# Short products of constants ahead of the small products of a chunked recurrence

## The chip, the core and the metric

The kernel runs on one core of one Trainium2 chip. The metric is the device time of one execution in microseconds. A core has a matrix engine (TensorE, PE in the profile, its weight loads PEld), three engines for elementwise work (VectorE: DVE, ScalarE: ACT, GpSimd: POOL) and a queue that issues the transfers (SyncE: SP). Each engine works through its own instructions in order and waits on semaphores for the others. PE writes only to PSUM, which is cut into banks of 512 float32 columns; before a bank is written again, what stands in it must have been read.

## What is computed

One step of a decoder layer for 576 tokens (64 of 8 short samples and 512 of a prompt): a norm, one wide projection, two kinds of token mixer side by side (a state-space mixer, and RWKV-7 with 16 heads of 64), an output projection, a gated feed-forward block, and an embedding per layer. The change touches the RWKV-7 part, whose recurrence is

```
def wkv_scan(r, decay, k, v, kk, a, s0):
    ...
    def step(s, inp):
        r_t, w_t, k_t, v_t, kk_t, a_t = inp
        s_kk = jnp.einsum('bhvk,bhk->bhv', s, kk_t)
        s = (s * w_t[:, :, None, :] - s_kk[..., None] * (kk_t * a_t)[:, :, None, :]
             + v_t[..., None] * k_t[:, :, None, :])
        return s, jnp.einsum('bhvk,bhk->bhv', s, r_t)

    s_fin, out = lax.scan(step, s0.astype(f32), seq)
```

All products are in float32 accuracy: a large one is split into a high and a low part of both operands and run as three products (L213 to L215).

## The kernel before

The 576 columns are cut into 9 chunks of 64 (chunk 0 holds the samples), and the 16 heads into four quarters of four heads: two pairs (`jj`) of two heads (`e`), the two heads of a pair in the upper and lower 64 partitions. For each quarter the kernel runs these steps.

- `prep` (L509): the decays, the normalised keys and the scaled operands `G` and `BK`. Its `by_channel` (L489) turns a factor per token into one per channel with PE transposes (L503, L506) into a bank `cb` (one buffer) or, in `head_norm`, `cx` (two buffers).
- `start_states` (L706): loads the samples' states and multiplies them with chunk 0's operands into `cb` (L714), 32 small products for each pair.
- `gram` (L581): the products of all operands within a chunk (L593), in five groups; a group fills a tile `lin` of two banks (two buffers), and DVE, ACT and POOL mask and copy it out (L603 to L618).
- `solve` (L632): inverts 72 triangular blocks with 60 dependent operations on DVE (L654, L656), between transfers through DRAM.
- `combine` (L661): puts the blocks' inverses together with 64 products of 32 x 32 (L678, L692) in two tiles `cx`.
- `chain` (L719): nine steps `core` (L769, L777, L782), `prompt_state` (L801) and `outp` (L792), each step needing the state of the one before it.
- `head_norm` (L866): centres the output (L879), sums its squares by token (L476) and scales it.

Beside this, `fill` takes projections off a list: each is 48 wide products of 288 columns (L213 to L215) into a `lin` tile. A projection is written where the quarter's steps call for it, but a scheduler orders all instructions of an engine by its own model of their times when the program is built; so wide products come to stand between the small ones of the chain. Tiles with one or two buffers decide when a product can start: the tile before it in the same buffer must have been read.

`gmask` is a constant of 128 x 128 ones and zeros in bfloat16 (L145), `blk` and `ident` are float32 constants.

Of the kernel before, what the change touches and what calls it, by code (L numbers as in the profile page):

```python
# [56 lines left out]
    return [8 + 2 * q, 9 + 2 * q, 2 * q, 2 * q + 1, 16 + 2 * q, 17 + 2 * q]  # L57


CONV_BC = [8, 9, 10, 11]  # L60
CONV_X = [0, 1, 2, 3, 4, 5, 6, 7]

# [12 lines left out]
def hybrid_step(ctx, tc, A):  # L75
# [168 lines left out]
    sst = se.tile([P, 26, 9], F32, tag="sst", name="sst")  # L244
    nc.sync.dma_start(sst[:], A["s_shift"])
    sho = se.tile([P, 26, 9], F32, tag="sho", name="sho")

    def cx_ps():
        return bank(sq_, "cx", 2)
# [239 lines left out]
    def by_channel(rn, jj, psum, tag):  # L489

        rnv = rn[:].rearrange("p (w h) -> p w h", w=5)[:, :, jj * 2:jj * 2 + 2].unsqueeze(3)
        if tag:
            rx = sp.tile([P, 5, 2, 64], F32, tag=tag, name=nm(tag), bufs=1)
            V.tensor_copy(rx[:], rnv.to_broadcast([P, 5, 2, 64]))
            rx4 = rx[:, 4]
        else:
            rx = slot("rx", [P, 4, 2, 64])
            V.tensor_copy(rx[:], rnv[:, 0:4].to_broadcast([P, 4, 2, 64]))
            rx4 = s2.tile([P, 2, 64], F32, tag="rx4", name=nm("rx4"))
            V.tensor_copy(rx4[:], rnv[:, 4].to_broadcast([P, 2, 64]))  # L500
        ps = psum()
        for w, a in enumerate(WIN[:4]):
            T.transpose(ps[:, a:a + P], rx[:, w].rearrange("p a b -> p (a b)"), ident[:])  # L503
        yield 0, 448, ps[:, 0:448]
        ps = psum()
        T.transpose(ps[:, 0:P], rx4.rearrange("p a b -> p (a b)"), ident[:])  # L506
        yield 448, NT, ps[:, 0:P]

# [72 lines left out]
    def gram(s):  # L581

        s.Lst = s2.tile([P, 9, 2, 64], F32, tag="Lst", name=nm("Lst"))
        for gs in ((0,), (1, 2), (3, 4), (5, 6), (7, 8)):
            n = len(gs)
            gl = slice(gs[0], gs[0] + n)
            mk = dgmask if gs[0] == 0 else gmask
            ps = lin.tile([P, 1024], F32, tag="lin", name=nm("lin"))
            for i, g in enumerate(gs):
                for jj in jj2:  # L590
                    for e in range(2):
                        c = e * 512 + (2 * i + jj) * 128
                        T.matmul(ps[:, c:c + 128].rearrange("p (a t) -> p a t", a=2),  # L593
                                 s.BK[jj][H[e], g].rearrange("p a t -> p (a t)"),
                                 s.G[H[e], g, jj, :, e], start=True, stop=True)
# [65 lines left out]
    def combine(s):  # L661
# [3 lines left out]
        for e in range(2):  # L665
            for z in range(2):
# [3 lines left out]
            nc.sync.dma_start(AA[e * 64:e * 64 + 32].rearrange("s g j t -> s (g j) t"),  # L670
                              s.Ad[e].rearrange("g s t -> s g t"))
        Wp = cx_ps()
        Wv = Wp[:].rearrange("p (g j t) -> p g j t", g=8, j=2)
        for g in range(1, 9):
            for jj in jj2:
# [4 lines left out]
        for e in range(2):  # L680
# [3 lines left out]
            else:  # L684
                V.tensor_scalar(AA[hi_:hi_ + 32, 1:9], Wv[hi_:hi_ + 32], -1.0, None, ALU.mult)
        Xp = cx_ps()
        Xv = Xp[:].rearrange("p (g j t) -> p g j t", g=8, j=2)
        for g in range(1, 9):
            for jj in jj2:
# [16 lines left out]
    def start_states(s):  # L706

        S0 = load_states(s)
        Zp = cb_ps()
        Zv = Zp[:, 0:256].rearrange("p (j a t) -> p j a t", j=2, a=2)  # L710
        for jj in jj2:
            for b in range(8):
                for e in range(2):
                    T.matmul(Zv[H[e], jj, :, b * 8:b * 8 + 8], S0[H[e], b, jj, :],  # L714
                             s.G[H[e], 0, jj, :, e, b * 8:b * 8 + 8], start=True, stop=True)
        s.Z = sp.tile([P, 2, 2, 64], F32, tag="Z", name=nm("Z"))
        act(s.Z[:], Zv)

    def chain(s):  # L719
# [45 lines left out]
        def core(g):  # L765
# [6 lines left out]
            V.tensor_copy(xs[H[1]], xw[H[1], :, 1])  # L772
            ups = cx_ps()
            uw = ups[:].rearrange("p (j v) -> p j v", j=8)
            for jj in jj2:
                for e in range(2):
                    T.matmul(uw[H[e], jj, :], TT[H[e], g, jj, :], xs[H[e], jj, :], start=True, stop=True)  # L777
# [747 lines left out]
```

## Time and profile before

| | us |
|---|---|
| timed runs, median of 3 | 1366.8 (1364.27 to 1370.2) |
| profiled execution, its own time | 1370.43 |
| span of its trace, first to last instruction | 1368.7 |
| mean granted clock of TensorE | 0.947 of full |
| first quarter's gram ends, combine begins | 138.7, 190.4 |
| first chain, first to last step begins | 198.9 to 305.5 |
| second chain | 349.8 to 450.8 |
| third chain | 486.1 to 563.6 |
| fourth chain | 595.8 to 671.2 |

The steps of the chains are found in the trace by L769, those of the gram by L593, those of the combine by L678 and L692, each four times over. Behind 671 us the state-space mixer and the output projection end, and from about 825 us on there are only wide products. A plain float32 product stands in the trace as two rows, one of the split kind as one. A row's duration holds the way through the array as well, so two rows in a row overlap; what a product costs in a stream is the distance of two starts. `PEclk` is the share of full speed that the clock of TensorE was granted.

### The profile page before, as it was taken

The page shows a single profiled execution, that of the slowest core. Times are in us where ns is not written, and L with a number is a line of the kernel's source. Part 1 is how long each engine was busy: PE and PEld are TensorE (multiplying, and loading weights), DVE is VectorE, ACT ScalarE, POOL GpSimd, SP SyncE. Part 2 cuts the span into 40 slices and gives each one's busy share as a digit, 9 for nine tenths or more (in the row PEclk, how much of TensorE's full clock was granted, in tenths as well). Part 3 has the DMA queues.
Part 4 walks back from the last instruction along what each step waited for, and adds up shares of the span by engine and source line. Part 5 has one row for each costly group of instructions (what it writes and reads, how often), then busy time and mean ns, then how long its engine had stood idle before and what let it go on. Part 6 is the DMA issues. An engine that isn't in the chain of part 4 may idle for free.

```text
span 1368.7 us, 26325 instructions
## 1 busy us (share of the span) xinstructions
PE 1259.1 (92%) x10565; PEld 1160.4 (85%) x10565; DVE 719.6 (53%) x1333; ACT 577.4 (42%) x1148; POOL 550.2 (40%) x543
## 2 busy tenths in 40 slices
PE   6897999999989979899989979999999999999986
PEld 5786897789868857777779769999999999999985
DVE  7648766787687785843367676522222221111255
ACT  6565345634653553344425364432332332222253
POOL 5326414632454153133456676432332332334332
PEclk9997899899979989989999989999999999999998
DMA  4322342234223312362644532233232222222432
GB/s 162 124 70 62 85 119 60 81 100 128 61 90 91 101 58 84 88 209 82 189 145 142 183 97 71 70 85 79 84 85 81 83 85 77 82 80 79 148 92 69
DMA packets 94458, 135.56 MB, mean 99 GB/s; under 512 B 34704, under 2 KB 39056, under 8 KB 94336
## 3 DMA queue, kind: packets, MB, share of 16 engines
q1 hardware_dynamic: 94336, 133.88, 32.8%
q8 instruction: 83, 1.36, 0.4%
q14 instruction: 39, 0.32, 0.1%
HBM read 106.10 MB, written 27.75 MB: 98 GB/s over the span
## 4 chain that ended last, share of the span: by engine, by line
PE 60%; DVE 15%; ACT 5%; DMA 5%; issue 4%; POOL 3%; DVEq 0%; SPq 0%; ACTq 0%; POOLq 0%
PE lin L215 16%; PE lin L213 16%; PE lin L214 16%; DVE h L375 2%; DVE Tt L656 1%; DVE tmp L654 1%; DMA raw<-wts 1%; POOL wlo L198 1%; DVE suv L809 1%; PE cx L777 1%; PE lin L593 1%; PE cx L769 1%; DVE wlo L198 1%; PE cx L792 1%; DVE pg L1373 1%
## 5 line engine op out<-in xcount | busy, mean ns | idle before, releaser
L213 PE MATMUL lin<-xhi,whi 128*128 128x288 f32 (+1 forms) x1488 | 450.8, 303 | 3.3 <-ACT whi L92 2.2
L215 PE MATMUL lin<-xhi,wlo 128*128 128x288 f32 (+1 forms) x1488 | 447.9, 301 | 3.2 <-POOL wlo L198 2.2
L214 PE MATMUL lin<-xlo,whi 128*128 128x288 f32 (+1 forms) x1488 | 447.7, 301 | 1.0 <-POOL xlo L186 1.0
L198 POOL TENSOR_TENSOR wlo<-raw,whi 128x512 fp32r<-128x512 f32 x136 | 182.8, 1344 | 501.9 <-ACT whi L92 462.1
L92 ACT ACTIVATE whi<-raw 128x512 fp32r<-128x512 f32 (+1 forms) x272 | 168.8, 621 | 397.7 <-PE lin L214 341.1
L213 PEld LDWEIGHTS lin<-xhi,whi 128*128 128x128 f32 (+1 forms) x1488 | 281.4, 189 | 10.5 <-ACT whi L92 2.6
L215 PEld LDWEIGHTS lin<-xhi,wlo 128*128 128x128 f32 (+1 forms) x1488 | 282.3, 190 | 7.0 <-POOL wlo L198 2.8
L214 PEld LDWEIGHTS lin<-xlo,whi 128*128 128x128 f32 (+1 forms) x1488 | 281.9, 189 | 6.1 <-POOL xlo L186 2.1
L198 DVE TENSOR_TENSOR wlo<-raw,whi 128x512 fp32r<-128x512 f32 (+1 forms) x136 | 98.4, 724 | 167.4 <-ACT whi L92 164.8
L215 PE MATMUL lin<-ah,wlo 128*128 128x288 f32 x352 | 105.0, 298 | 0.9
L213 PE MATMUL lin<-ah,whi 128*128 128x288 f32 x352 | 104.0, 296 | 0.0
L214 PE MATMUL lin<-al,whi 128*128 128x288 f32 x352 | 103.8, 295 | 0.0
L215 PEld LDWEIGHTS lin<-ah,wlo 128*128 128x128 f32 x352 | 66.2, 188 | 3.2 <-POOL wlo L198 2.6
L214 PEld LDWEIGHTS lin<-al,whi 128*128 128x128 f32 x352 | 66.1, 188 | 0.0
L213 PEld LDWEIGHTS lin<-ah,whi 128*128 128x128 f32 x352 | 66.0, 187 | 0.0
L1332 DVE TENSOR_TENSOR sg<-lin,sg 128x576 f32<-128x576 f32 x22 | 16.7, 758 | 82.9 <-PE lin L215 81.7
L1327 DVE TENSOR_TENSOR sg<-lin,rstd 128x576 f32<-128x576 f32 x22 | 16.7, 758 | 69.3 <-PE lin L215 69.0
L654 DVE TENSOR_TENSOR tmp<-L,Tt 72x30 f32<-72x30 f32 (+14 forms) x120 | 48.9, 407 | 3.2
L656 DVE TENSOR_TENSOR Tt<-Tt,tmp 72x30 f32<-72x30 f32 (+14 forms) x120 | 46.1, 384 | 3.4
L213 PE MATMUL lin<-xu,whi 128*128 128x288 f32 x128 | 39.9, 313 | 8.5 <-ACT xu L92 6.9
L215 PE MATMUL lin<-xu,wlo 128*128 128x288 f32 x128 | 40.0, 314 | 7.3 <-DVE wlo L198 5.5
L186 POOL TENSOR_TENSOR al<-sg,ah 128x576 fp32r<-128x576 f32 x22 | 31.5, 1433 | 32.1 <-ACT ah L92 32.1
(370 smaller groups left out, 2513.6 us busy)
## 6 DMA issues: line engine op xcount, KB each, us to landing
raw<-wts SPq DMA_DIRECT2D x271, 256.0 KB, 2.6
S<-s_wkv SPq DMA_DIRECT2D x8, 512.0 KB, 5.1
hd<-s_ssm SPq DMA_DIRECT2D x8, 512.0 KB, 4.0
o_ssm_s<-hd SPq DMA_DIRECT2D x8, 512.0 KB, 2.9
xbc_d<-E SPq DMA_DIRECT2D x12, 288.0 KB, 2.1
x<-xT SPq DMA_DIRECT2D x8, 288.0 KB
gate_d<-g SPq DMA_DIRECT2D x8, 288.0 KB, 2.6
bv_d<-rw SPq DMA_DIRECT2D x8, 288.0 KB
```

The lines of the kernel that those rows point to most:

```text
L92: S.activation(out, in_, func, bias=bias, scale=scale)
L186: eng.tensor_tensor(lo[:], src, hi[:].bitcast(F32), ALU.subtract)
L198: eng.tensor_tensor(lo[:, 0:n], raw[:, 0:n], hi[:, 0:n].bitcast(F32), ALU.subtract)
L213: T.matmul(ps[:, a:b], whi, xhi[:, a:b], start=first, stop=False)
L214: T.matmul(ps[:, a:b], whi, xlo[:, a:b], start=False, stop=False)
L215: T.matmul(ps[:, a:b], wlo, xhi[:, a:b], start=False, stop=last)
L375: V.scalar_tensor_tensor(h[:], E[:, i:i + 600], w(i), h[:], ALU.mult, ALU.add)
L593: T.matmul(ps[:, c:c + 128].rearrange("p (a t) -> p a t", a=2), s.BK[jj][H[e], g].rearrange("p a t -> p (a t)"), s.G[H[e], g, jj, :, e], s ...
L654: V.tensor_tensor(o, L[:, jx:jx + 1, jx + 1:32].to_broadcast([NB, jx, n]), Tt[:, 0:jx, jx:jx + 1].to_broadcast([NB, jx, n]), ALU.mult)
L656: V.tensor_tensor(Tt[:, 0:jx, jx + 1:32], Tt[:, 0:jx, jx + 1:32], o, ALU.subtract)
L1327: V.tensor_tensor(s_[:], ps, rs[:], ALU.mult)
L1332: V.tensor_tensor(s_[:], up, s_[:], ALU.mult)
```

## The change

A helper `beat` multiplies `gmask` with a column of itself, spread over 512 columns, and writes the result into a tile that is about to be written by the step's own products; these begin with `start=True` and overwrite it. It has no operand that anything computes late, so it waits only for the tile's bank. The helper is called ahead of both sets of transposes in `by_channel` (one beat each), of each gram group (ten ahead of the first quarter's first group, two ahead of its others, three and one in the other quarters), of both products of `combine` (two each), of the states' products (two, and two of 256 columns between the pairs), and of the second product of the third quarter's last two chain steps (two each). That makes 107 products.

```
+BEATS = [(10, 2), (3, 1), (3, 1), (3, 1)]
...
+    def beat(ps, n=1, w=512):
+
+        for _ in range(n):
+            T.matmul(ps[:, 0:w], gmask[:].rearrange("p a b -> p (a b)"), gmask[:, 0, 0:1].to_broadcast([P, w]),
+                     start=True, stop=True)
...
         ps = psum()
+        beat(ps, 1)
         for w, a in enumerate(WIN[:4]):
             T.transpose(ps[:, a:a + P], rx[:, w].rearrange("p a b -> p (a b)"), ident[:])
         yield 0, 448, ps[:, 0:448]
         ps = psum()
+        beat(ps, 1)
         T.transpose(ps[:, 0:P], rx4.rearrange("p a b -> p (a b)"), ident[:])
...
             ps = lin.tile([P, 1024], F32, tag="lin", name=nm("lin"))
+            beat(ps, BEATS[s.q][bool(gs[0])])
             for i, g in enumerate(gs):
...
         Wp = cx_ps()
+        beat(Wp, 2)
...
         Xp = cx_ps()
+        beat(Xp, 2)
...
+        beat(Zp, 2)
         for jj in jj2:
+            if jj:
+                beat(Zp[:, 256:512], 2, 256)
             for b in range(8):
...
             ups = cx_ps()
             uw = ups[:].rearrange("p (j v) -> p j v", j=8)
+            if q == 2 and g > 6:
+                beat(ups, 2)
             for jj in jj2:
```

The scheduler decides where a beat stands, and it moves other products too. Three places on PE follow; in the changed kernel the beat is L252, and the other line numbers are 7 to 18 higher (L593 is L603, L714 is L729, L678 is L689, L503 is L511, L213 to L215 are L214 to L216).

First, PE in the second quarter, where the states' products into `cb` meet the first gram products into `lin`, before:

```order
L714 MATMUL cb_3081<-G_2686,S_456_3079 64x2x8 x17
L792 MATMUL cx_1824<-G_982,suv_1768 64x64
L714 MATMUL cb_3081<-G_2686,S_456_3079 64x2x8 x15
L593 MATMUL lin_3117<-G_2686,bk_2849 128x128
L801 MATMUL cx_1840<-suv_1768,bkt_1811 64x64 x4
L792 MATMUL cx_1824<-G_982,suv_1768 64x64 x3
L593 MATMUL lin_3132<-G_2686,bk_2849 128x128 x2
```

and the same place on PE after the change:

```order
L252 LDWEIGHTS gmask
L252 MATMUL cb_3119<-gmask 128x256
L729 MATMUL cb_3119<-G_2720,S_456_3117 64x2x8
L809 MATMUL cx_1854<-G_982,suv_1798 64x64
L729 MATMUL cb_3119<-G_2720,S_456_3117 64x2x8 x5
L818 MATMUL cx_1870<-suv_1798,bkt_1841 64x64 x4
L809 MATMUL cx_1854<-G_982,suv_1798 64x64 x3
L729 MATMUL cb_3119<-G_2720,S_456_3117 64x2x8 x10
L603 MATMUL lin_3159<-G_2720,bk_2885 128x128
L252 LDWEIGHTS gmask
L252 MATMUL lin_3177<-gmask 128x512
L603 MATMUL lin_3177<-G_2720,bk_2885 128x128 x2
```

The beats stand between the two pairs' products and ahead of the group's first product; a weight load of `gmask` stands as a row of its own.

Second, PE in the head norm of the second quarter, where the second pair's factors are transposed into `cx` (`rxg` is the factor per token; `ulh` and `ull` belong to the small projections of the fourth quarter's preparation), before:

```order
L213 MATMUL lin_6071<-ulh_345,whi_5973 128x288
L503 MATMUL cx_3824<-ident,rxg_3822 128x128 x4
L506 MATMUL cx_3830<-ident,rxg_3822 128x128
L214 MATMUL lin_6071<-ull_346,whi_5973 128x288
L215 MATMUL lin_6071<-ulh_345,wlo_5974 128x288
```

and after the change:

```order
L252 LDWEIGHTS gmask
L252 MATMUL cx_3879<-gmask 128x512
L214 MATMUL lin_5984<-xhi_456,whi_6017 128x288
L252 LDWEIGHTS gmask
L252 MATMUL cx_3886<-gmask 128x512
L215 MATMUL lin_5984<-xlo_457,whi_6017 128x288
L216 MATMUL lin_5984<-xhi_456,wlo_6018 128x288
L214 MATMUL lin_5984<-xhi_461,whi_6017 128x288
L215 MATMUL lin_5984<-xlo_462,whi_6017 128x288
L216 MATMUL lin_5984<-xhi_461,wlo_6018 128x288
L511 MATMUL cx_3879<-ident,rxg_3877 128x128 x4
L515 MATMUL cx_3886<-ident,rxg_3877 128x128
```

Before, the projections from the layer's input (`xhi`, `xlo`) were through by then and only the small ones (`ulh`, `ull`) were left; now the former stand there. Counted over the whole of PE's order, 128 products of 288 columns (L213 to L215) stand between the last step of the second chain and the first of the third before, and 194 after; behind the first step of the third chain there are 12 more (of the small projections); between the last step of the first chain and the last step of the second there are 78 fewer.

Third, PE at the combine of the fourth quarter (`AA` and `Lst` are its operands), before:

```order
L503 MATMUL cx_5547<-ident,rxg_5545 128x128 x4
L506 MATMUL cx_5553<-ident,rxg_5545 128x128
L740 MATMUL tr_6735<-ident,rw_5893 128x128
L740 MATMUL tr_6735<-ident,rw_5961 128x128
L678 MATMUL cx_6545<-AA_6538,Lst_6153 32x32 x32
```

and after:

```order
L511 MATMUL cx_5629<-ident,rxg_5627 128x128 x4
L515 MATMUL cx_5636<-ident,rxg_5627 128x128
L764 MATMUL tr_6791<-ident,bk_6136 128x128
L764 MATMUL tr_6791<-ident,bk_6193 128x128
L755 MATMUL tr_6838<-ident,rw_5977 128x128
L755 MATMUL tr_6838<-ident,rw_6045 128x128
L252 LDWEIGHTS gmask
L252 MATMUL cx_6644<-gmask 128x512
L252 LDWEIGHTS gmask
L252 MATMUL cx_6644<-gmask 128x512
L689 MATMUL cx_6644<-AA_6637,Lst_6245 32x32 x32
```

Two beats stand between the last transposes and the combine's first product, and two of the transposes (L764) have moved behind the head norm's.

More of the change, by code (lines that the diff above doesn't have):

```diff
@@ L246, in hybrid_step, with beat @@
     sho = se.tile([P, 26, 9], F32, tag="sho", name="sho")
+    def beat(ps, n=1, w=512):
+        for _ in range(n):
+            T.matmul(ps[:, 0:w], gmask[:].rearrange("p a b -> p (a b)"), gmask[:, 0, 0:1].to_broadcast([P, w]),
+                     start=True, stop=True)
     def cx_ps():
@@ L501, in by_channel @@
         ps = psum()
+        beat(ps, 1)
         for w, a in enumerate(WIN[:4]):
@@ L672, in combine @@
         Wp = cx_ps()
+        beat(Wp, 2)
         Wv = Wp[:].rearrange("p (g j t) -> p g j t", g=8, j=2)
@@ L686, in combine @@
         Xp = cx_ps()
+        beat(Xp, 2)
         Xv = Xp[:].rearrange("p (g j t) -> p g j t", g=8, j=2)
@@ L774, in core @@
             uw = ups[:].rearrange("p (j v) -> p j v", j=8)
+            if q == 2 and g > 6:
+                beat(ups, 2)
             for jj in jj2:
```

6 lines of the change are left out of this document (added).

## The prediction

> **What bounds the kernel now.** I read four views in this order: the page, the busy time by stretch, the chain of waits, and the order of time at a few places. The page first.
>
> ```profile
> span 1368.7 us, 26325 instructions
> PE 1259.1 (92%) x10565; PEld 1160.4 (85%) x10565; DVE 719.6 (53%) x1333; ACT 577.4 (42%) x1148; POOL 550.2 (40%) x543
> PEclk9997899899979989989999989999999999999998
> PE 60%; DVE 15%; ACT 5%; DMA 5%; issue 4%; POOL 3%; DVEq 0%; SPq 0%; ACTq 0%; POOLq 0%
> ```
>
> TensorE (PE) is busy for 92% of the span and holds 60% of the chain that ended last, so it is the bound. But its clock is not whole everywhere: PEclk dips to 7 to 9 tenths in the first half, which is the stage of the recurrence, and hardly at all behind it. The change touches only that stage. So I look at it in stretches. A row has the stretch, its length, the busy time of PE, PEld, DVE, ACT and POOL, the granted clock, and the DMAs.
>
> ```profile
> 41.40:44.80 3.40, 0.00 (x0) 0.00 (x0) 3.40 (x9) 3.01 (x4) 0.28 (x1) 1.00 0.00 0
> 249.60:253.00 3.40, 3.40 (x83) 3.12 (x82) 3.32 (x6) 3.26 (x7) 1.75 (x3) 1.00 0.28 95
> 253.00:256.40 3.40, 2.55 (x11) 1.60 (x10) 3.27 (x7) 1.65 (x6) 3.32 (x5) 0.50 0.28 81
> 474.90:478.30 3.40, 1.96 (x13) 1.25 (x11) 2.14 (x5) 3.31 (x7) 1.41 (x1) 1.00 0.00 0
> 478.30:481.70 3.40, 3.00 (x63) 2.77 (x65) 3.40 (x6) 2.79 (x6) 0.83 (x3) 1.00 0.16 60
> ```
>
> From 249.6 to 253.0 PE is busy all of the time, with 83 small products, and the 3.4 us behind run at 0.50. From 474.9 to 478.3 it is busy for 1.96 us only, with 13 products, most of them 288 columns wide, and the clock behind stays at 1.00. So here it is not being busy that keeps the clock, but how many columns stream through the array within some 3.4 us. Thirteen products of at most 288 columns are 3744 columns; a beat of 512 is a seventh of that. So, as an estimate, a stretch without anything needs up to seven beats, and one that nearly holds needs one or two.
>
> The Trainium skill states a rule that differs: its page "TensorE: Matmul & The Clock Gate" (Part 1: The HAM clock gate) has the clock halved after at least one idle window of about 3.4 us and full again after a busy one. The length agrees with the rows above, and 41.4 to 44.8 is such an idle window; the stretch from 249.6, wholly busy and followed by 0.50, does not agree. What that rule would make of the change is the last rival.
>
> What half the clock costs is seen where one group of products is on the chain of waits at both clocks (start, us, engine, tile, line, count):
>
> ```profile
> 401.54 2.01 PE lin L593 x16
> 407.49 1.09 PE lin L593 x16
> 343.11 1.15 PE cx L678 x64
> 587.51 1.92 PE cx L678 x64
> ```
>
> The 16 products of a gram group take 2.01 us at half and 1.09 us at full clock, the 64 of the combine 1.92 and 1.15. I take half of PE's time on the chain as what the whole clock gives back.
>
> How much PE there is on the chain in the slow stretches: first the chain's shares within six of them, in this order: 123.3 to 140.4 (first quarter's gram), 253.0 to 266.7 (second's), 386.1 to 406.6 (third's), 519.2 to 526.1 (fourth's state and gram products), 563.6 to 570.4 (end of the third chain), 584.1 to 594.3 (fourth's combine).
>
> ```profile
> by line: DVE h L375 26.8%; ACT G L92 19.5%; DMA xbc_d<-E 12.3%; PE lin L593 12.3%; DVE Lst L603 10.6%; POOL G L618 7.0%; POOL G L614 6.7%; ACT h L92 5.2%; DVE lo L575 4.5%; DVE E L380 4.1%; issue 3.4%; DVE E L381 0.8%; POOLq L614 0.2%; ACTq
> by line: DVE h L375 25.3%; DVE suv L809 16.5%; PE lin L593 14.6%; DVE lo L561 12.8%; DVE lo L575 5.5%; PE cx L777 5.0%; DVE E L380 4.4%; PE cx L801 3.4%; issue 3.2%; PE cx L782 3.2%; PE cx L792 2.9%; ACT suv L92 2.8%; DVE E L381 2.7%; DVE x
> by line: PE lin L593 17.5%; issue 15.7%; DVE h L375 11.9%; DVE E L381 8.0%; DVE suv L809 5.1%; DVE bk L564 4.7%; PE cx L792 4.4%; PE cx L769 4.2%; DVE pb L556 3.7%; DVE lo L561 3.7%; DVE lo L575 3.5%; PE cx L801 3.4%; PE tr L740 3.0%; ACT s
> by line: DMA S<-s_wkv 51.7%; PE cb L714 48.1%; PE lin L593 29.1%; PE cx L777 10.3%; PE cx L782 6.8%; PE cx L792 3.3%; issue 0.6%
> by line: PE cx L879 19.7%; PE cx L769 18.2%; PE cx L777 14.9%; PE cx L792 12.5%; PE cx L801 9.8%; DVE ar L880 6.9%; PE cx L782 6.4%; ACT gsq L92 6.2%; ACT ar L92 4.2%; ACT xs L92 4.1%; issue 2.7%
> by line: PE lin L213 19.4%; PE cx L678 18.8%; PE lin L214 16.2%; PE lin L215 14.1%; ACT L92 12.6%; PE cx L503 8.5%; DVE ar L890 6.8%; PE tr L749 6.8%; ACT thz L92 6.4%; ACT bkt L92 2.8%; issue 1.2%
> ```
>
> Summing each row's PE shares and multiplying by its length (pieces that reach over an edge count whole, which overstates a little) gives 12.3% of 17.1 = 2.1 us, 29.1% of 13.7 = 4.0, 32.5% of 20.5 = 6.7, 97.6% of 6.9 = 6.7, 81.5% of 6.8 = 5.5 and 83.8% of 10.2 = 8.5: together 33.5 us, of which the full clock would give back half, 16.8. Four more slow stretches of 3.4 us are wholly busy, the first and the last of them being
>
> ```profile
> 143.80:147.20 3.40, 3.40 (x16) 3.26 (x15) 1.89 (x2) 0.00 (x0) 3.21 (x4) 0.50 0.55 178
> 423.70:427.10 3.40, 3.40 (x17) 3.29 (x16) 3.03 (x12) 1.03 (x3) 0.00 (x0) 0.50 0.17 64
> ```
>
> each worth 1.7 us, 6.8 in all. So **23.6 us** is the most that the clock can give back in this stage.
>
> **What the change adds, and its price.** It adds 107 products of a constant with itself, 99 of 512 columns and 8 of 256; it removes nothing and adds no DMA. Such a bfloat16 product is not in the trace. The nearest row is a single-pass one of 512 columns; two of them, and the row behind:
>
> ```profile
> 738.43 0.62 PE L1141 MATMUL d<-xe,bm 128*128 128x512 f32 x2
> 738.89 0.29 PE L213 MATMUL lin<-xhi,whi 128*128 128x288 f32 x1
> 709.79 0.86 PE d L1076 x2
> ```
>
> From 738.43 to 738.89 the two take 0.46 us, 0.23 each. A plain float32 product of the same width, which runs as two passes, takes 0.86 us, which I keep as the upper end of a beat that goes slower than I think (at half clock too); the lower end is nothing, for a beat that stands in a wait. I take 0.23, since a beat is one row in the order, as L1141 is. All 107 on the path would cost 99 x 0.23 + 8 x 0.12 = 23.7 us.
>
> Most are not on it. A beat waits only for its bank, so it starts when the bank's last reader is done, and fills the wait for the operands behind it. What is queued behind it on PE waits too, so a beat is free only as far as PE idles there.
>
> - The four beats of the first quarter's combine have banks that are free from the start; the scheduler puts them right behind the first transposes of the reciprocal norm, ahead of a product that waited 1.58 us (row below). Four beats are 0.9 us: nothing.
> - The first quarter's gram, state products and transposes (ten beats at once, then twos): their stretch has PE busy for 11.6 of 17.1 us and PE holds 12.3% of its chain. Hidden but for the two transposes that stand in a full stretch.
> - In stretches that are wholly busy at full clock each beat is paid: 2 there, 3 in the second quarter's transposes, 8 in the first head norm and second combine (row from 325: 24.85 of 25 us busy), 2 behind it, and half of those in the second and third head norms with their combines and the last head norm (8, 10 and 4, where PE idles for part): 4 + 5 + 2. That is 26, or 6.0 us.
> - The last three gram groups of a quarter wait for a bank that ACT has to empty, and then their beats stand between the release and the product: 6 + 3 + 3 + 3 = 15 beats, 3.4 us.
>
> ```profile
> 30.16 0.37 PE L213 MATMUL lin<-xu,whi 128*128 128x288 f32 x1 [1.58 <-DVE u L341]
> 325.00:350.00 25.00, 24.85 (x344) 23.67 (x341) 12.91 (x25) 13.40 (x31) 6.68 (x5) 1.00 0.47 136
> 450.00:475.00 25.00, 24.97 (x254) 22.96 (x253) 17.16 (x44) 12.41 (x28) 4.04 (x4) 1.00 0.48 128
> 475.00:500.00 25.00, 18.14 (x235) 14.55 (x233) 21.25 (x34) 18.46 (x36) 9.98 (x14) 0.73 0.11 35
> 560.20:563.60 3.40, 0.55 (x15) 0.41 (x13) 3.22 (x8) 0.94 (x3) 1.04 (x1) 1.00 0.37 127
> 580.70:584.10 3.40, 1.50 (x12) 1.10 (x10) 1.67 (x3) 3.33 (x6) 1.74 (x2) 1.00 0.92 256
> ```
>
> **Which slow stretches go.** The window ahead decides. Ahead of 253.0 it was close, and five beats or their halves come there: 2.0 us. Ahead of 386 no beat does much, but the scheduler moves 52 wide products of the projections there, between the third and the fifth step of the second quarter's chain: half of 6.7, 3.3 us. Ahead of 584.1 PE streamed 12 products in 1.50 us and the change has eight beats around there: 4.3. At 560.2 only 0.55 us of 3.4 are busy and four beats come within the last two steps, at 515 to 519 four: I count half, 1.4 and 1.7, and half at the first gram, 0.5. Of the four single stretches one: 1.7. Sum 14.9, say **-15 us**.
>
> **What else the order does.** The scheduler shifts the wide products of the projections: between the end of the first quarter's chain and the last step of the second's 78 fewer stand, and in and right behind the second head norm 78 more. There the rows at 450 and 475 show the cover end: PE goes from 24.97 to 18.14 busy while DVE goes from 17.16 to 21.25 of 25 us. With the products beside the head norm, the head norm's DVE work falls ahead of 475 and what is late next is DVE and POOL in the fourth quarter's preparation. At 0.13 us a product the 78 are 10 us of PE work; at most the 6.9 us that PE idles from 475 to 500 can be had. I take 4, with nothing and 7 as ends.
>
> **The sum:** -15 (clock) - 4 (order) + 9 (6.0 + 3.4 of beats) = -10 us, against the profiled execution's own 1370.4 us. The median of the timed runs is 1366.8, 3.6 below, so I give 1366.8 - 10 = **1357**. About 0.5%, 6.8 us, is what a measurement of this kernel can tell from no change.
>
> **The rivals.**
> 1. *More windows hold than I count.* A window that keeps its clock feeds the next. All 23.6 us of clock and 7 of order come back, with 9 paid: -22, 1345. For it: most of the slow stretches follow each other without a break. Against it: in the first gram DVE, ACT and POOL hold over 70% of the chain.
> 2. *The clock comes back and nobody waits for it.* Where DVE holds the chain (solve, the convolution of L375, the preparation), a faster gram product only waits earlier: clock -9, order 0, beats +9: 1367. For it: from 123 to 140 and from 253 to 267 the largest shares are DVE h L375.
> 3. *The beats stand behind the release and miss the threshold.* In grams 2 to 4 one beat a group is too little to hold the clock; it then runs at half speed, 0.43 us, ahead of a product that its bank held up. The 21 beats of those grams and the 16 of the state products (8 of them half as wide, so 33 in all) would be paid at that price, 14 us, with 6 of the full stretches, and the clock would give back half of what I count: 14 + 6 - 7.5 - 4 = +9, 1376. It decides if less than about half of the slow time goes while those beats are on the path.
> 4. *Only standing still loses the clock.* Then the one window that counts is 41.4 to 44.8, no beat stands there, the slow stretches have another cause and stay, and the beats' 9 us are paid: 1376. The stretch from 249.6 speaks against it; by the chain as shown it is unlikely. The Trainium skill's page "TensorE: Matmul & The Clock Gate" (Why this matters for your kernels) asks only that no gap of PE be longer than some 3 us, which would come out this way.
>
> **Chances.** Forecast 0.46, of which 0.05 ends within 0.5%; rival 1 0.17; rival 2 0.20; rival 3 0.13; rival 4 0.04. Faster by over 0.5%: 0.41 + 0.17 = 0.58. Within: 0.05 + 0.20 = 0.25. Slower: 0.17. The range has the forecast with its ends and rival 2, and the nearer part of rivals 1 and 3: 1340 to 1372.
>
> **What would show it.** Right: at 253, 386 and 584 the granted clock stays at 1.00 and the 16 products of L593 (its number moves by ten lines) take 1.1 us; the beats take 0.23 us each; PE is busier from 475 to 500. Wrong: the same number of slow stretches with beats in them at 0.43; gram products that wait for beats; a chain of waits that is DVE's to a larger share with the same span. If the stage up to the last chain step ends no earlier, the order's 4 us were a shift and no gain.

## The result and the profile after

The changed kernel takes 1384.03 us (median of 4, 1383.34 to 1388.08), the kernel before 1367.78 beside it (1364.27 to 1370.2): a ratio of 1.0127, with 1.0108 to 1.0146 as its 95% interval. It is 16 us slower; forecast were 10 us faster, and 1340 to 1372 as the range. The profiled execution took 1383.34 us.

The page of the changed kernel, the lines that answer to those of before:

```profile
span 1381.6 us, 26520 instructions
PE 1284.9 (93%) x10672; PEld 1168.1 (85%) x10672; DVE 711.9 (52%) x1333; ACT 578.8 (42%) x1148; POOL 543.7 (39%) x543
PEclk9998999899989987899999989999999999999998
PE 70%; DVE 15%; ACT 6%; issue 3%; DMA 3%; POOL 2%; SPq 0%; DVEq 0%; ACTq 0%; POOLq 0%
```

With the 107 beats and the new order PE's busy time rises by 25.8 us, its share of the chain goes from 60% to 70%, and the dips of PEclk have moved and not gone. DVE's share has stayed.

I cut the span at the first product of the last chain step (L769 before; the numbers move by up to 17 lines, so L784 now). Up to there is the stage that the change touches. The busy time by stretch, before: the stage, the rest, the third chain from its second to its sixth step, and the second quarter's gram and state products.

```profile
0.00:671.17 671.17, 598.49 (x5435) 524.85 (x5435) 458.72 (x929) 329.96 (x707) 259.61 (x321) 0.92 0.33 100
671.17:1368.70 697.53, 660.61 (x5133) 635.58 (x5131) 260.89 (x404) 247.41 (x441) 290.56 (x222) 0.98 0.33 98
497.04:527.75 30.71, 25.54 (x286) 18.64 (x285) 18.75 (x40) 12.34 (x35) 15.92 (x17) 0.86 0.17 55
242.76:266.96 24.20, 22.82 (x232) 19.19 (x230) 19.45 (x36) 13.77 (x33) 14.00 (x21) 0.72 0.20 63
```

The same view of the changed kernel: the stage, the same part of the third chain, the longest slow stretch, and 475 to 500.

```profile
0.00:684.80 684.80, 625.35 (x5537) 534.16 (x5538) 454.99 (x929) 330.55 (x707) 254.22 (x321) 0.92 0.33 98
491.75:536.37 44.62, 38.50 (x292) 25.91 (x292) 25.96 (x50) 19.88 (x46) 18.02 (x21) 0.66 0.14 44
512.00:535.90 23.90, 23.05 (x204) 18.54 (x206) 10.13 (x28) 7.57 (x22) 6.22 (x9) 0.50 0.10 32
475.00:500.00 25.00, 21.18 (x298) 15.14 (x298) 19.50 (x33) 16.96 (x34) 8.48 (x11) 0.90 0.35 104
```

The stage is 13.6 us longer. PE's idle time in it (length less busy) fell from 72.7 to 59.5 us, so the beats did fill waits; but PE is busy for 26.9 us more. The part of the third chain took 30.7 us and takes 44.6, and inside it PE is busy for 23.05 of 23.90 us at 0.50. Below, "half-clock time" is the time that the clock's records of the trace show at half speed; in the stage it was 112.6 us and is 116.1. PE is busy for a part of it only, 95.8 us before and 102.5 after. Half of that part is what the clock costs on a busy PE; busy time less this half is called "PE work" below, the time that PE would be busy at the whole clock: 550.6 us before, 574.1 after.

### The profile page after: what moved, and what is told of

Same layout as the page of the kernel before. It is cut to its first block, busy times and chain, and to the rows that moved or that the text cites. A ratio compares the mean times of both kernels' runs of the same rounds, so it can differ in the third digit from the quotient of the medians.

```text
span 1381.6 us, 26520 instructions
## 1 busy us (share of the span) xinstructions
PE 1284.9 (93%) x10672; PEld 1168.1 (85%) x10672; DVE 711.9 (52%) x1333; ACT 578.8 (42%) x1148; POOL 543.7 (39%) x543
## 4 chain that ended last, share of the span: by engine, by line
PE 70%; DVE 15%; ACT 6%; issue 3%; DMA 3%; POOL 2%; SPq 0%; DVEq 0%; ACTq 0%; POOLq 0%
PE lin L216 18%; PE lin L214 18%; PE lin L215 17%; PE lin L603 2%; DVE Tt L666 1%; DVE wlo L199 1%; PE cx L794 1%; DVE tmp L664 1%; ACT whi L93 1%; PE cx L784 1%; DVE h L382 1%; PE cx L809 1%; POOL wlo L199 1%; DMA raw<-wts 1%; PE cx L844 1%
## 5 line engine op out<-in xcount | busy, mean ns | idle before, releaser
L214 PE MATMUL lin<-xhi,whi 128*128 128x288 f32 (+1 forms) x1488 | 451.8, 304 | 4.8 <-ACT whi L93 2.7
L215 PE MATMUL lin<-xlo,whi 128*128 128x288 f32 (+1 forms) x1488 | 448.4, 301 | 1.3 <-POOL xlo L187 1.3
L216 PE MATMUL lin<-xhi,wlo 128*128 128x288 f32 (+1 forms) x1488 | 448.6, 302 | 0.6 <-DVE wlo L199 0.3
L214 PEld LDWEIGHTS lin<-xhi,whi 128*128 128x128 f32 (+1 forms) x1488 | 281.8, 189 | 13.9 <-ACT whi L93 3.5
L215 PEld LDWEIGHTS lin<-xlo,whi 128*128 128x128 f32 (+1 forms) x1488 | 281.7, 189 | 6.7 <-POOL xlo L187 2.3
L216 PEld LDWEIGHTS lin<-xhi,wlo 128*128 128x128 f32 (+1 forms) x1488 | 282.3, 190 | 5.2 <-issue 0.8
L216 PE MATMUL lin<-ah,wlo 128*128 128x288 f32 x352 | 105.0, 298 | 1.0
L214 PE MATMUL lin<-ah,whi 128*128 128x288 f32 x352 | 104.0, 296 | 0.0
L215 PE MATMUL lin<-al,whi 128*128 128x288 f32 x352 | 103.8, 295 | 0.0
L216 PEld LDWEIGHTS lin<-ah,wlo 128*128 128x128 f32 x352 | 66.2, 188 | 3.2 <-POOL wlo L199 2.6
L215 PEld LDWEIGHTS lin<-al,whi 128*128 128x128 f32 x352 | 66.1, 188 | 0.0
L214 PEld LDWEIGHTS lin<-ah,whi 128*128 128x128 f32 x352 | 66.0, 188 | 0.0
L666 DVE TENSOR_TENSOR Tt<-Tt,tmp 72x30 f32<-72x30 f32 (+14 forms) x120 | 49.8, 415 | 3.2
L216 PE MATMUL lin<-xu,wlo 128*128 128x288 f32 x128 | 39.9, 313 | 7.2 <-DVE wlo L199 5.4
L214 PE MATMUL lin<-xu,whi 128*128 128x288 f32 x128 | 39.9, 313 | 6.7 <-ACT xu L93 6.6
L664 DVE TENSOR_TENSOR tmp<-L,Tt 72x30 f32<-72x30 f32 (+14 forms) x120 | 42.8, 357 | 3.1
L603 PEld LDWEIGHTS lin<-G,bk 64*128 64x128 f32 x288 | 31.0, 260 | 15.5 <-issue 10.2
## 6 DMA issues: line engine op xcount, KB each, us to landing
raw<-wts SPq DMA_DIRECT2D x271, 256.0 KB, 2.6
S<-s_wkv SPq DMA_DIRECT2D x8, 512.0 KB
hd<-s_ssm SPq DMA_DIRECT2D x8, 512.0 KB
o_ssm_s<-hd SPq DMA_DIRECT2D x8, 512.0 KB, 2.6
```

Source lines behind the costliest of these rows:

```text
L214: T.matmul(ps[:, a:b], whi, xhi[:, a:b], start=first, stop=False)
L215: T.matmul(ps[:, a:b], whi, xlo[:, a:b], start=False, stop=False)
L216: T.matmul(ps[:, a:b], wlo, xhi[:, a:b], start=False, stop=last)
L664: V.tensor_tensor(o, L[:, jx:jx + 1, jx + 1:32].to_broadcast([NB, jx, n]), Tt[:, 0:jx, jx:jx + 1].to_broadcast([NB, jx, n]), ALU.mult)
L666: V.tensor_tensor(Tt[:, 0:jx, jx + 1:32], Tt[:, 0:jx, jx + 1:32], o, ALU.subtract)
```

## The experiments

The change does two things: it adds beats, and it makes the scheduler order everything anew. The program that the scheduler returns is a list of instructions with their waits, so each can be had alone: beats can be taken out of the finished list (their waits pass to the next product) or put into it.

All runs, each ratio against runs of before on the same chip. Stage, PE busy, idle and half-clock time (us) are of the one profiled execution, up to the last chain step; "waits" are beats put where PE stands still. In e8, e9, e10, e12 and e13 5 to 23 records of beats are missing from the trace, so that their busy time is up to some 5 us too low and their idle time as much too high.

| kernel | median us | ratio (95%) | stage | PE busy | idle | half-clock |
|---|---|---|---|---|---|---|
| before | 1367.8 | 1 | 671.2 | 598.5 | 72.7 | 112.6 |
| changed | 1384.0 | 1.0127 (1.0108-1.0146) | 684.8 | 625.4 | 59.5 | 116.1 |
| e1 order alone | 1378.2 | 1.0103 (1.0063-1.0143) | 679.0 | 609.1 | 70.0 | 136.5 |
| e2 beats alone | 1378.6 | 1.0100 (1.0069-1.0130) | 679.1 | 618.7 | 60.5 | 99.0 |
| e3 order, -127 | 1384.3 | 1.0118 (1.0082-1.0155) | 680.0 | 608.3 | 71.7 | 119.5 |
| e4 order, -27 | 1390.6 | 1.0166 (1.0131-1.0200) | 690.6 | 615.6 | 75.0 | 146.8 |
| e5 order, +45 | 1400.0 | 1.0228 (1.0188-1.0268) | 694.7 | 615.7 | 79.0 | 153.6 |
| e6 beats of 1 column | 1369.1 | 1.0021 (0.9999-1.0042) | 668.1 | 601.0 | 67.1 | 109.2 |
| e7 order, gram first | 1382.6 | 1.0120 (1.0090-1.0151) | 676.7 | 607.1 | 69.7 | 133.1 |
| e8 the same with beats | 1387.6 | 1.0146 (1.0113-1.0180) | 686.5 | 620.9 | 65.5 | 116.1 |
| e9 beats x3, one quarter | 1370.9 | 1.0030 (1.0012-1.0049) | 668.9 | 600.1 | 68.8 | 92.2 |
| e10 waits, order of before | 1363.9 | 0.9973 (0.9954-0.9993) | 667.3 | 608.8 | 58.5 | 58.0 |
| e11 before, once more | 1375.2 | one run | 674.1 | 604.0 | 70.1 | 126.3 |
| e12 waits, changed order | 1369.6 | 1.0010 (0.9990-1.0031) | 663.5 | 612.0 | 51.5 | 51.2 |
| e13 waits, order +45 | 1392.9 | 1.0194 (1.0164-1.0224) | 686.5 | 632.1 | 54.4 | 78.5 |
| e14 as e10, whole program | 1361.1 | 0.9956 (0.9939-0.9972) | 661.6 | 608.5 | 53.1 | 54.6 |
| e15 as e12, whole program | 1363.8 | 0.9975 (0.9960-0.9990) | 667.8 | 620.7 | 47.1 | 64.9 |

### Order alone, beats alone (e1, e2)

e1 takes the beats out of the changed kernel's finished program:

```diff
+                if i.debug.bass_funcname.endswith("beat"):
...
+                        waits += i.sync_info.on_wait
...
+                    continue
```

> The changed kernel's order of instructions on every engine, with the 107 beats taken out of it behind the scheduler (their waits pass to the next product). Theory A, the scheduler's new order costs the time (the fourth quarter's preparation starts some 9 us later because the wide products of the projections were moved ahead of it): as slow as the changed kernel or slower, 1380 to 1392 us, with the third chain's sixth step again 8 us later than before. Theory B, the beats themselves cost it (they stand behind the release of a bank, many at half the clock): back at 1368 or a few us below. Theory C, both: about halfway, 1374 to 1378.

e2 puts them into the finished program of before, ahead of the first product that overwrites the bank:

```diff
+        if k in first:
+            name, col, n, w = first[k]
...
+            for _ in range(n):
...
+                new.append(mybir.InstMatmult(name="I-%d" % (1000001 + 2 * num), engine=PE, debug=i.debug, start_tensor_calc=True,
...
+                                             sync_info=mybir.SyncInfo(on_wait=waits, on_update=[])))
...
+        new.append(i)
```

> The order of before, instruction by instruction, with the same 107 beats put in behind the scheduler, each group right ahead of the first product that overwrites its bank and waiting for that bank alone. Theory A (order): faster than before, by my forecast's own terms -15 of clock and +9 of beats, so 1358 to 1364 us. Theory B (beats): 1378 to 1386, with the products of a gram group waiting for beats of 0.43 us. Theory C (both): 1372 to 1376. The granted clock in the recurrence tells whether beats hold it when nothing is moved: under A the half-clock time falls from 148 us to about 100, under B it stays.

Measured were +13.6 and +13.9 us. e2 is where B had it, e1 is not, and A fails for e2; C's times are missed too: each half costs nearly what both cost together. The stretches of e1, the stage and the part of the third chain:

```profile
0.00:679.01 679.01, 609.05 (x5435) 533.17 (x5436) 457.50 (x929) 330.57 (x707) 254.53 (x321) 0.90 0.32 99
488.39:531.45 43.06, 37.43 (x282) 26.66 (x282) 25.64 (x49) 18.97 (x44) 18.07 (x21) 0.59 0.13 42
```

PE runs the same 5435 products as before and is busy for 10.6 us more, while half-clock time rises by 23.9. Its busy time at half the clock goes from 95.8 to 117.0 us, and half of that rise is 10.6: PE work is 550.6 us in both. Idle time falls by 2.7. So what the order adds to the stage in these two profiles, 7.8 us, is PE running slowly. The timed runs say the same: the mean granted clock of e1's four is 0.938 and of the seven of before beside them 0.947. With records of 1 and 0.5 only, that is some 24 us more at half the clock in an execution. The third chain's part is 43.1 us without any beat: its loss is the order's. It holds nearly the same products (286 and 282 rows), and busy time times granted clock is the same in both, 25.54 x 0.86 and 37.43 x 0.59, about 22 us.

The stage of e2, the part of the third chain in it, and, from its order of time, PE at the third group of the first gram:

```profile
0.00:679.13 679.13, 618.68 (x5538) 527.63 (x5539) 456.27 (x929) 330.39 (x707) 258.62 (x321) 0.93 0.33 99
506.45:534.16 27.71, 25.14 (x294) 17.02 (x293) 19.09 (x41) 12.16 (x36) 15.71 (x17) 0.95 0.19 62
```

```profile
134.66 1.03 PE L603 MATMUL lin<-gmask 128*128 128x512 bf16 x2 [1.56 <-ACT G L93]
135.62 0.80 PE L603 MATMUL lin<-G,bk 64*128 64x128 f32 x4
```

Here PE stands still for 1.56 us until ACT has emptied the bank; the beats wait for that too, and then run for 1.03 us, at half the clock, ahead of the products. The wait is ahead of the beats and not behind them.

### What a beat costs (e6)

Against the kernel of e2:

```diff
-            name, col, n, w = first[k]
+            name, col, n, w = first[k][:3] + (1,)
```

> The order of before with the 107 beats put in ahead of their products as in the run of the beats alone (1378.6 us, +13.9), but each one column wide: the weight load and the wait for the bank stay, the streaming goes. Theory B1, a beat costs what it streams, because PE is busy where it stands: back at 1365 to 1369. Theory B2, the bank wait and the weight load cost it, by whatever stands behind them: 1373 to 1379.

1369.1, at the upper edge of B1. Since e6 and e2 have one order and the same waits, their difference is the streaming. The stage is 11.0 us longer in e2, PE is busy for 17.7 us more and idle time is 6.7 less. PE's busy time at half the clock is 88.3 us and not 93.2; with half of the difference (2.5) added back, the streaming is 20.1 us of PE work: 6.7 went into waits, 2.5 came back by the clock, 11.0 was paid.

### Other orders (e3, e4, e5)

The scheduler makes another order when some beats are left out of the source. In each of these one call or one quarter is left out, and the rest are then taken out as in e1:

```diff
-        beat(ps, 1)
+        pass
```

> An order that the scheduler makes when the beats ahead of the first transposes are left out of the source; the other 91 beats are then taken out behind the scheduler, so no beat runs. Here 127 wide products fewer stand ahead of the last step of the second chain (78 in the changed kernel's order). Theory A1, the wide products that go behind the second head norm delay the fourth quarter's preparation: slower than the order with 78, so 1380 to 1388 us. Theory A2, any other order than that of before costs about the same, by no one cause: 1372 to 1380, the same as the next two.

> As the run before, with the order that comes out when the second quarter's beats are left out of the source; 27 wide products fewer stand ahead of the last step of the second chain; no beat runs. Theory A1: a third of the order's loss of 13.6 us, so 1367 to 1371. Theory A2: 1372 to 1380.

> As the two runs before, with the order that comes out when the beats ahead of the second transposes are left out; here 45 wide products more stand ahead of the last step of the second chain, and 91 more ahead of the eighth step of the third; no beat runs. Theory A1: not slower than before, 1358 to 1367 us. Theory A2: 1372 to 1380.

1384, 1391 and 1400. The first is where A1 had it, but the other two are slower than either theory allows, and the loss does not follow the number of products moved. A1 falls, and A2's "about the same" too. (In e5 the 91 products more stand ahead of the seventh step; ahead of the eighth there are 38 more.) What goes with the loss better is the mean granted clock of the timed runs, 0.939, 0.934 and 0.928 in these, 0.938 in e1 and 0.947 before. That it is the cause is not shown by this: half-clock time in the stage is less in the profile of e3 than in that of e1, and e12 and e13 below part the two.

### State products behind the gram groups (e7, e8)

In the order of before, three of the fourth quarter's five gram groups stand ahead of its state products (L714), in the changed one only the first and the beginning of the second.

```diff
...
-        start_states(s)
+        if s.q != 3:
+            start_states(s)
         gram(s)
+        if s.q == 3:
+            start_states(s)
```

The copy of their result into `G` moves with them. In both runs these products read chunk 0's operands after the gram has overwritten them, so the states' part in the fourth quarter's samples is another; the amount of work is the same.

> The changed kernel's order with one thing put back: in the fourth quarter the state products are written behind the gram groups (as they stood in the order of before), the wide products stand where the change put them (78 fewer ahead of the last step of the second chain); the beats are taken out behind the scheduler. Theory A3, the order costs because the fourth quarter's state products came ahead of its gram groups and made one run of small products at half the clock on a busy PE: the four third-chain steps from the second to the sixth, 43.1 us in the order alone and 30.7 before, fall to 31 to 35, and the time from 1378.2 to 1364 to 1370. Theory A4, it costs because the wide products moved: it stays at 1375 to 1381, those steps at 41 to 45.

> The same order as the run before, with the 107 beats in it. By the two runs of one order with and without beats so far (before's order: +13.9 us; the changed order: 1384.0 against 1378.2, +5.8) it is 5 to 14 us above the run before: 1370 to 1382 under theory A3, 1381 to 1392 under A4.

1382.6 and 1387.6: A3 falls. The part of the third chain came down from 43.1 to 39.5 us only, and the time not at all. That the wide products did it, as A4 has it, is not shown by this either: both of A4's ranges for e7 are missed by some 1.5 us, and no run moved these products alone.

### Enough beats to hold the clock (e9)

```diff
+        if cur[0] != 1:
+            return
+        n *= 3
```

> The order of before, with beats only in the second quarter's preparation, state products and gram groups, three times as many as in the change there (39 of 512 columns, 6 of 256; 9.7 us of PE work at 0.23 and 0.12). With the simple number the stretch from 253.0 ran at half the clock for 13.7 us before and for 10.2 with the beats alone. Theory D1, beats hold the clock once they are many enough, at a price on a busy PE that eats what comes back: half-clock time there 0 to 3.4 us, the second chain's start 2 to 6 us later than before, 1367 to 1373 us. Theory D2, more beats hold no more: it stays at 10 or more, start 8 to 11 us later, 1373 to 1378. Theory D3, more beats pay: start earlier than before, 1360 to 1365.

The second quarter's gram and state products in e9:

```profile
240.82:266.44 25.62, 24.22 (x262) 17.69 (x263) 18.75 (x36) 13.77 (x33) 12.42 (x21) 1.00 0.18 58
```

D1. The clock, 0.72 there before, is 1.00, and the stretch takes 25.62 us in place of 24.20: the beats that hold the clock cost what it gives. The second chain starts 1.0 us later than before (D1 said 2 to 6). At the change's own number it did not hold: in e2 the clock is at half for 10.2 us there, in the changed kernel from 256.0 to 269.7.

### Beats where PE stands still (e10, e11)

The profile of before says where PE waits. Into 33 waits of 0.45 us and more come as many beats as fit, into banks whose last tile has been read, so that no beat is to wait for anything:

```diff
+            nth[key] = nth.get(key, 0) + 1
+            n = waits.get((key, nth[key]), 0)
...
+                for _ in range(n):
...
+                                                 sync_info=mybir.SyncInfo(on_wait=waits_, on_update=[])))
...
+WAITS = {(213, 145): 1, (213, 165): 6, (213, 340): 6, (213, 671): 3, (215, 177): 3, (215, 361): 4,
```

> The order of before with 136 beats of 512 columns put where TensorE stood still in the profile of before: ahead of 33 instructions that waited 0.45 to 3 us between 86 and 586 us, as many as the wait holds at 0.23 us each, into banks that are read out by then, so that no beat waits. Theory E1, place: a beat in a wait costs nothing and holds the clock of the window behind, which the change's beats, ahead of the product that overwrites their bank, did not get: half-clock time in the recurrence falls from 112.6 us to 60 to 80, time 1350 to 1360. Theory E2, the clock returns and nobody waits for it: half-clock time falls, time 1362 to 1368. Theory E3, with beats in them the waits move and the beats are paid: 1370 to 1380.

> The kernel of before, unchanged, for a second profile: how far two executions of one program differ by themselves. If the half-clock windows are fixed by the order, they come at the same places to the microsecond; if the grid of windows starts at another point in each execution, single windows come and go, and the stage up to the last chain step differs by 1 to 4 us.

One such place, PE in order of time, before:

```profile
516.64 0.61 PE L769 MATMUL cx<-suv,G 128*128 128x128 f32 x4
519.53 1.04 PE L714 MATMUL cb<-G,S 64*64 64x16 f32 x16 [2.28 <-DMA S<-s_wkv]
```

and in e10:

```profile
512.53 0.61 PE L769 MATMUL cx<-suv,G 128*128 128x128 f32 x4
513.19 1.90 PE L714 MATMUL cx<-gmask 128*128 128x512 bf16 x8
515.02 0.76 PE L714 MATMUL cb<-G,S 64*64 64x16 f32 x20
```

The stage of e10 in the view by stretch:

```profile
0.00:667.30 667.30, 608.76 (x5549) 519.80 (x5572) 458.65 (x929) 329.15 (x707) 261.21 (x321) 0.96 0.34 100
```

Eight beats take 1.90 us of a wait of 2.28, and the state products behind them run at the whole clock: 20 of them in 0.76 us, where 16 took 1.04. Half-clock time fell from 112.6 to 58.0 us, a little further than E1 said, but the time by 0.27% only, as E2 said (1362 to 1368): of the 27 us that the clock gives back at most, the stage shows 3.9.

e11 shows how far one program differs by itself: the chain steps up to the third chain's last one keep their lengths within 0.4 us, but the first quarter has 41.0 us at half the clock and not 30.7, PE is busy in the stage for 5.5 us more and the stage is 3.0 us longer. Differences of that size in one profile prove nothing.

### Is it the clock? (e12, e13, e14, e15)

The same in the changed order (e12) and in the slowest of the four (e13), from the waits in the profiles of e1 and e5, here against the kernel of e1:

```diff
     strip(nc)
+    fill_waits(nc, WAITS)
     r = _run(nc, [arrays], core_ids=[0]).results[0]
```

> The changed kernel's order, its own 107 beats taken out (1378.2 us without any), and 144 beats put where TensorE stood still in the profile of that order: ahead of 38 instructions that waited 0.45 us or more up to 600 us, as many as each wait holds, into banks that are read out by then. In the order of before such beats took the half-clock time up to the last chain step from 112.6 to 58 us and the time down by 0.27%. Theory F1, the new order costs by the clock (136.5 us at half the clock in that stage against 112.6): with the clock held it comes close to that kernel of 1363.9 us, 1362 to 1369. Theory F2, the new order costs by what it makes late, whatever the clock: the clock gives back 4 us as it did in the order of before, 1372 to 1377.

> The same for the slowest of the four orders (45 wide products more ahead of the last step of the second chain; 1400.0 us without beats, 153.6 us at half the clock up to the last chain step): 174 beats ahead of 34 waiting instructions. Theory F1: half-clock time under 90 us and the time 1366 to 1382. Theory F2: 1392 to 1399.

The stage and the third chain's part in e12:

```profile
0.00:663.47 663.47, 611.95 (x5555) 519.28 (x5579) 454.85 (x929) 329.99 (x707) 256.15 (x321) 0.96 0.34 101
484.25:519.22 34.97, 28.76 (x292) 18.41 (x294) 24.97 (x47) 18.57 (x43) 17.70 (x21) 0.95 0.16 55
```

For the changed order it is F1, if just past the edge of its range (1369.6): the part of the third chain goes from 43.1 to 35.0 us at 0.95, the stage from 679.0 to 663.5. For e13 it is F2: half-clock time halves, the time falls by 7 us only and 27 remain, although its granted clock, 0.952 in the mean of its timed runs, is above that of before, 0.947. Most of that order's loss has another reason, which I did not follow.

e14 and e15 fill the waits behind the last chain step too.

> The order of before with beats in TensorE's waits as in the run that came to 1363.9 us, now over the whole program: 218 beats ahead of 51 waiting instructions, 82 of them behind the last chain step, where the profile of before has 29.4 us at half the clock. Theory F1 (time at half the clock on a busy PE is paid at half, wherever it is): another 5 to 10 us off, 1354 to 1360. Theory F2 (behind the last chain step nobody waits for the clock): 1362 to 1366.

> The changed kernel's order with beats in its waits over the whole program, 223 ahead of 56 waiting instructions. With them up to 600 us it came to 1369.6 us: its stage up to the last chain step ended 7.7 us earlier than in the profile of before (663.5 against 671.2), but 42.4 us at half the clock followed behind it, against 29.4. Theory F1: those go and the earlier end is kept, 1354 to 1362. Theory F2: 1366 to 1370.

The stretch behind the last chain step, in e14 and then in e15:

```profile
661.59:1359.10 697.51, 674.64 (x5217) 639.14 (x5215) 261.38 (x404) 246.98 (x441) 290.93 (x222) 0.99 0.33 98
```

```profile
667.82:1361.30 693.48, 669.52 (x5208) 634.28 (x5206) 258.57 (x404) 248.36 (x441) 291.09 (x222) 0.99 0.33 99
```

Both times lie between the theories. That the clock is paid behind the last chain step too is not shown: in e14 that stretch takes as long as before (697.51 and 697.53 us), so that its profile's gain lies wholly in the stage; in e15 it takes 693.5 us where it took 703.0 in e12, but the stage is 4.4 us longer than there. e14 is 0.44% below before, the fastest of all.

The mean granted clock of the timed runs is 0.964 in e10 and 0.963 in e12, and 0.972 in both e14 and e15. With the clock thus alike, the changed order stands 5.7 us (e12 and e10) and 2.7 us (e15 and e14) behind that of before; without beats it was 13.6. So by the medians the clock is 8 to 11 us of the order's loss. The intervals are wide, e1's alone is from 0.63% to 1.43%, and they allow anything from some 2 us to the whole. What is left, 3 to 6 us by the medians, stays open.

## Why the prediction was wrong, point by point

**The bound and the price: right.** PE is the bound. Beats of the changed kernel, in order of time, and two pieces of its chain at half the clock:

```profile
115.59 2.33 PE L252 MATMUL lin<-gmask 128*128 128x512 bf16 x10
```

```profile
530.62 0.54 PE lin L252
531.16 2.01 PE lin L603 x16
```

Ten take 2.33 us, 0.23 each, as estimated. At half the clock one takes 0.54 us of the chain, more than the 0.43 of rival 3 and less than the 0.86 that was kept as the upper end. All 107 are 23.5 us of PE work in the changed kernel's stage (574.1 less 550.6), where 23.7 was estimated. "The 16 products take 1.1" failed here: they take 2.01, with a beat ahead of them.

**The order, "-4, with nothing and 7 as ends": wrong, and the largest miss.** Alone it costs 13.6 us, 8 to 11 of them by the clock as far as the medians tell. The forecast read the 78 moved products as work that fills PE's idle time at 475 to 500. They do: PE is busy for 21.18 of these 25 us, where it was 18.14, and in e1 the stage's idle time is 2.7 us less, near the 4. What failed is the other side of it: what the new order does to the clock was put at nothing, without a reason, except at 386, where it helped. From 512.0 to 535.9 there are only products of at most 128 columns and four beats, on a busy PE at 0.50. A row of the prediction (249.6 to 253.0, wholly busy, then 0.50) had shown that a dense run of small products can lose the clock. Which of the moves made this run is not shown: between the second and the sixth step of the third chain no projection product of 288 columns stands in either order, and with the state products put back (e7) the part still took 39.5 us. The prediction's own mark for being wrong was that the stage ends no earlier; in e1 the second chain's last step starts 10.4 us earlier than before, and the sixth step of the third chain 3.7 later.

**The beats on the path, "+9": mis-sized.** Between e1 and the changed kernel, with one order, idle time falls by 10.5 us, PE's busy time at half the clock goes from 117.0 to 102.5, and PE is busy for 16.3 us more: 16.3 + 7.3 = 23.6 us of beats, of which 13 found no wait. In the order of before (before and e2) it is 23.9 less 12.2, about 12. "A beat is free only as far as PE idles there" was right; counted as idle was what lay somewhere in a stretch (first gram, state products, transposes), not what lay between the release of the beat's bank and the release of the product's operands. In the changed kernel three of the 107 are followed by over 0.1 us of idle time.

**The clock, "-15": about -4 with nothing moved (before and e2), -7 in the changed order, and with the order's own +10.6 it came to +3.** Of the named stretches the second gram stays slow for 13.7 us; at 386 it is 13.7 in place of 20.5, where wide products had come; the fourth quarter's is 23.9 in place of 6.9; the end of the third chain 13.6 in place of 6.8; the combine 6.9 in place of 10.2. One to three beats for a group were too few for the second gram, where three times as many held the clock (e9). The 23.6 us called the most leave out three slow stretches of before (44.8 to 51.6, 99.4 to 102.8 and 485.1 to 498.8) without a reason.

**The rivals.** Rival 3 had the mechanism of the beats: behind the release, at half the clock, too few for the threshold; its 1376 is close to the beats alone, 1378.6. But it too took the order as a gain. No rival had the order as a loss, and that is why the range missed. Rival 2's point, that nobody waits for the clock, is what e10 showed in the order of before. Rival 4 is out: from 512.0 to 535.9 the clock stays at half on a PE that hardly stands still, and e10 holds the clock with beats in waits that were all shorter than 3 us.

**The sum.** In the stage, by the profiles: +7.8 for the order (+10.6 of clock, -2.7 of idle) and +5.8 for the beats (+13.1 unhidden, -7.3 of clock) are the +13.6 of the changed kernel's stage. These sizes are of one profile each, and two profiles of before differ by 5.7 us in the same term of clock and 3.0 in the stage (e11). They also need not be those of the medians: the profiled execution of before was the slowest of its timed runs (1370.4), that of e1 among the fastest of its own (1375.3), so that they lie 4.8 us apart and the medians 13.6.

## What to carry to other kernels

On an engine that bounds a stage, filler is free only in a wait that lasts longer than the filler: what the products behind it wait for must come that much later than what the filler waits for. Take these places from the trace, instruction by instruction, and not from an engine's idle share of a stretch. Where a scheduler orders the program, an edit's new order is a second change: run the order without the edit and the edit in the old order, before either is believed. And of a new order ask where dense runs of small products come to stand: here one ran at half the clock for 23.9 us on a busy PE.

## What had not been expected of the hardware

Seven windows in a row at half the clock come with PE busy for 23.05 of 23.90 us (512.0 to 535.9 of the changed kernel). The Trainium skill's page "TensorE: Matmul & The Clock Gate" (Part 1: The HAM clock gate) gives back the whole clock after one busy window of about 3.4 us; this row does not agree. The page calls that window free-running, which agrees: the first slow stretch begins at 44.8 us in the profile of before and at 43.5 in that of e11, though PE's first product in it starts 0.13 us later there (46.12 and 45.99). Its first 3.4 us, before and then in e11:

```profile
44.80:48.20 3.40, 2.21 (x9) 2.21 (x10) 3.40 (x5) 1.71 (x5) 3.40 (x2) 0.50 0.26 80
```

```profile
43.50:46.90 3.40, 0.79 (x3) 0.79 (x4) 3.40 (x7) 2.26 (x5) 2.26 (x1) 0.50 0.01 2
```

One program's time goes with the clock it is granted: over 86 timed runs of before, 1359.9 to 1375.0 us, the correlation of time and mean granted clock is -0.73, about 8 us for 0.01. So kernels that differ by a few us had to be told apart by many runs and not by one profile.
